# A deep trunk in exact fp32 halves: one block's turn shared by two engines, high parts first, and two steps of the last head in another order

## The chip, the cores and the metric

One core of one Trainium2 chip. The metric is the device time of one execution in microseconds, lower is better. TensorE (PE) multiplies, ScalarE (ACT), VectorE (DVE) and GpSimd (POOL) do the elementwise work, SyncE (SP) and the other engines' queues start DMA transfers. The kernel before ran in 942.38 us, median of three runs.

## The reference

Two layers of a decoder trunk over `S` = 512 tokens of width `D` = 1024, in fp32. Layer 0 mixes tokens by causal pooling, layer 1 by causal differential attention; a SwiGLU feed-forward network (inner width 2816) follows each; every residual is normalized afterwards.

```python
for i in range(2):
    if i % 2 == 0:
        h = multiscale_pool(x, pool_w, pool_scale)      # means over 2, 4, 8, 16 tokens minus x, times 4 matrices
    else:
        h = diff_attention(x, w_qkv, w_o, lam_p, subln_g, rel_table, lambda_init)   # 8 heads, 2 maps each
    x = layernorm(ALPHA * x + h, ln_mix_g[i], ln_mix_b[i])
    x = layernorm(ALPHA * x + (silu(x @ w_gate[i]) * (x @ w_up[i])) @ w_down[i], ln_ffn_g[i], ln_ffn_b[i])
```

## The kernel before

**Products.** Each fp32 operand is divided into a high part (a cast to the fast matmul format, `fp32r`, on ScalarE) and a low part (operand minus high part, on VectorE): `split` (L116, its two instructions L123 and L124). `mm3` (L147) makes a product of three matmuls: high by high (L149), high by low (L150), low by high (L151). In the profile a matmul's row names its line and its two inputs; `w3h` and `w3l` are the high and low parts of weight row 3.

**Weights.** All weights lie in one array of rows of 128x1024. `fetch` (L107) loads rows on SP's queue into five buffers (`raw`), `ready(n)` (L126) divides all rows up to n: for each it fetches five rows ahead, casts and subtracts. Rows 0 and 1 are the pooling matrices; rows 2 to 5 (`w2` to `w5`) are the gate and up matrices of the first two pairs of the feed-forward network, rows 6 and 7 (`g_4`, `g_5`) those of the third. The rows of the output matrix `w_o` of attention are `w92` to `w99`.

**Order.** The whole kernel is written in program order: the schedule is manual, so each engine runs its own instructions in the order in which the lines below issue them, and waits by semaphores for the others. Eight PSUM banks (`bank`, L62) are handed out by the framework as they come free.

**Start and pooling layer (L281 to L490).** Seven warm matmuls of the identity (`warm`, L324; an fp32 matmul is two records in the profile) fill TensorE until data are there. Tokens lie in four blocks of 128. `low` (L368) multiplies block 0 and 1 by the pooling bands, for each of eight column blocks k in turn: high by high, high by low, low by high; `d` (L285) is the correction for the first 16 tokens. `mixed(s, d)` (L401) multiplies pooled block s by the pooling matrices, `summed(s, d)` (L419) adds the result to the residual (`residual`, L181) and takes the statistics of the half row (`stat`, L187), `spread_of` (L194) gets mean and factor (the power is GpSimd's, L199), and `norm` (L202) normalizes.

**The turn.** The feed-forward products need the tokens along the free axis: `transposed(n, s)` (L232) turns block s by eight transposes into two PSUM banks (`pt`), and `turned` (L241) takes each bank in turn: four activations with the norm's scale and bias per partition write `y` (L249), then `split` writes the high and low parts into `xt`. Column blocks 0 to 3 come from the first bank, 4 to 7 from the second.

**Hand-over to the feed-forward network.** After the turns of block 0 and 1, `ffn(0, ...)` (L502) starts products for three gate/up pairs on the first half of the tokens (blocks 0 and 1; `lo` = 0), each product 24 matmuls of 256 columns, and goes on with the second half (`lo` = 256). The turns of blocks 2 and 3 are put between the products of the first half by `late`: after product (0, 1) and after product (1, 0), where (f, i) is pair f, i = 0 for gate (`g`), 1 for up (`u`). `product` (L623) calls `mm3` for k = 0 to 7.

**The last head (L1339 to L1417).** Attention runs head by head: `scores`, `softmax` (L1154), `combine` (L1170, the difference of the two maps), then one head later `transposed`, `mix` (values, with a square on ScalarE for the head norm), `root` (L1218: Ln and Exp on ScalarE) and `scaled` (L1228: the head's output times its factor on VectorE, then its division into parts). After head 7, `gather` (L1235) multiplies the first four heads by the first four rows of `w_o` for the four blocks s, and between these run `root(6)`, the transposes and `mix` of head 7, and `root(7)`. At block 0 `ready` divides row `w96` and then `scaled(6)` runs; at block 3 `ready` divides `w98` and `w99` and then `scaled(7)` runs.

Of the kernel before, what the change touches and what calls it, by code (L numbers as in the profile page):

```python
# [54 lines left out]
def trunk(ctx, tc, x, wall, pscale, lam_p, subln, table, lng, lnb, band, first, onehot, out):  # L55
# [60 lines left out]
    def split(dst_h, dst_l, src, scale=1.0, low=None):  # L116
        if scale != 1.0:
            nc.scalar.mul(dst_h, src, scale)
            nc.vector.scalar_tensor_tensor(
                dst_l, src, scale, dst_h.bitcast(F32), op0=ALU.mult, op1=ALU.subtract  # L120
            )
        else:
            nc.scalar.copy(dst_h, src)  # L123
            (low or nc.vector).tensor_tensor(dst_l, src, dst_h.bitcast(F32), op=ALU.subtract)  # L124
# [116 lines left out]
    def turned(n, s, kept=None):  # L241
        for i, pt in enumerate(turns.pop((n, s))):
            if kept:
                y = kept[i][:, :, s % 2 * P : (s % 2 + 1) * P]
            else:
                y = keep.tile([P, 4, P], F32, tag="y", name=f"y{n}_{s}_{i}", bufs=2)
            for k in range(4):
                kk = 4 * i + k
                nc.scalar.activation(  # L249
                    y[:, k, :],  # L250
                    pt[:, k * P : (k + 1) * P],
                    AF.Identity,
                    bias=bT[:, n, kk : kk + 1],
                    scale=gT[:, n, kk : kk + 1],
                )
            o = (s % 2) * P
            split(*(xt[:, s // 2, j, 4 * i : 4 * i + 4, o : o + P] for j in range(2)), y)

    def turn(n, s):
        transposed(n, s)  # L260
        turned(n, s)
# [19 lines left out]
    with tc.tile_pool(name="pool", bufs=1) as pp:  # L281
# [39 lines left out]
        sch = pp.tile([1, D], F32R, name="sch")  # L321
        scl = pp.tile([1, D], F32R, name="scl")
        warm = bank("warm")
        for i in range(7):  # L324
            nc.tensor.matmul(warm[:, 0:P], ident, ident, start=True, stop=True)
        scb = []
        nc.vector.tensor_copy(fh[:, :, :BAND], bnd)
# [28 lines left out]
        def xk(t, s, k):  # L356
            return t[:, s, k * P : (k + 1) * P]
# [8 lines left out]
                mm(scb[c], one, scl[:, cc], start=False, stop=True)  # L366

        def low(t, ks):  # L368
            for k in ks:
                g = k // 2  # L370
                o = made[0, g][:, (k % 2) * 256 : (k % 2 + 1) * 256]
                if t == 0:
                    mm(o, xk(xnh, 0, k), fh[:, g, :], start=k % 2 == 0, stop=False)
                    mm(o, xk(xnh, 0, k), fl[:, g, :], start=False, stop=False)
                    mm(o, xk(xnl, 0, k), fh[:, g, :], start=False, stop=False)
                else:
                    mm(o, xk(xnh, 1, k), bh[:, g, 0:256], start=False, stop=False)
                    mm(o, xk(xnl, 1, k), bh[:, g, 0:256], start=False, stop=k % 2 == 1)

        def high(blocks, ks):  # L380
            for s in blocks:
# [71 lines left out]
        tbh = pp.tile([33, HEADS], F32R, name="tbh")  # L453
        tbl = pp.tile([33, HEADS], F32R, name="tbl")
        ohr = pp.tile([33, NEAR], F32R, name="ohr")
        split(tbh, tbl, tb)
        nc.scalar.copy(ohr, oh_)
        transposed(0, 0)
# [4 lines left out]
        mm(lines_bank[:HEADS], tbl, ohr, start=False, stop=True)  # L463
        summed(1, 0, 1)
        spread_of(0, 1)
        summed(2, 0)
        norm(0, 1)
        transposed(0, 1)
        mixed(3, 1)
        turned(0, 0)  # L470
        summed(2, 1)
        spread_of(0, 2)
        turned(0, 1)
        ready(4)
        summed(3, 0, 1)
        norm(0, 2)
        spread_of(0, 3)
        ready(5)
        norm(0, 3)
        ready(6)  # L480

        line = pp.tile([HEADS, LINE], F32, name="line")
        far = pp.tile([HEADS, 1], F32, name="far")
        nc.gpsimd.memset(line[:, NEAR:], 0.0)
# [17 lines left out]
    def ffn(layer, late):  # L502
# [5 lines left out]
        with tc.tile_pool(name=f"ffn{layer}", bufs=1) as fp:  # L508
# [111 lines left out]
                if upto > len(chunks):  # L620
                    prepare(upto - len(chunks), upto - len(chunks))

            def product(acc, j, lo, hi):  # L623
                h, l = halves[j]
                for k in range(KB):
# [163 lines left out]
            load_terms(0)  # L789
            load_terms(1)  # L790
            sums = sums_of_x()
            for lo in (0, 256):
                for f in range(early):
                    for i in range(2):
                        product(accs[f][i], 2 * f + i, lo, lo + 256)
                        if not lo and (f, i) in late:
                            late[f, i]()
                        if not lo:
                            advance(2 * early, True)
                    if lo:  # L800
# [199 lines left out]
    def attention():  # L1000
        n = 2
        with tc.tile_pool(name="attn", bufs=1) as ap:
# [337 lines left out]
            for h in range(HEADS):  # L1340
                if h > 0:
                    combine(h - 1, 3)
                if h > 0:
                    split_values(h - 1)
                if h == 0:
                    scalars()
                if 1 < h <= SB + 1:
                    affine(n - 1, h - 2)
                if h == SB + 2:
                    load_gb(n)  # L1350
                if h + 1 < HEADS:
                    load_bias(h + 1)
                if h > 0:
                    accs = [bank(f"{nm}{h}") for nm in "qk"]
                    w = take(2)
                    ready(where[0] + {1: 3, last: 3}.get(h, 1))
                    query(accs[0], w[0])
                    split_query(h, "q", accs[0])
                    if h > 1:
                        root(h - 2)  # L1360
                    query(accs[1], w[1])
                    ready(where[0] + {1: 4, last: 3}.get(h, 2))
                    if h > 1:
                        scaled(h - 2)
                    split_query(h, "k", accs[1])
                    if h == 1:
                        w = take(2)
                        for r in range(2):
                            values("Q3", r, vc, w[r])
                        for s in range(2):  # L1370
                            combined(part(0, 1, s), vc[s], part(0, 1, s), ALU.subtract)
                    transposed(h - 1)
                start_scores(h)
                scores(h, 0, 1)
                for q in range(2):
                    softmax(h, q)
                if h == 0:
                    for s in range(2):
                        combined(part(1, 1, s), vc[s], part(1, 1, s), ALU.subtract)
                for q in (2, 3):  # L1380
                    scores(h, q)
                if h > 0:
                    mix(h - 1)
                if h == last:
                    ready(where[0] + 4)
                for q in (2, 3):
                    combine(h, q - 2)
                    softmax(h, q)
                combine(h, 2)
            cw = where[0]  # L1390
            combine(HEADS - 1, 3)
# [142 lines left out]
```

## Time and profile before

| | |
|---|---|
| Runs | 942.38, 941.96, 943.63 us; median 942.38 |
| Profiled execution | 942.9 us, span from first to last instruction 941.1 us |
| TensorE busy | 926.7 us, 98% of the span, 5712 matmuls |
| VectorE busy | 786.9 us, 84% |
| ScalarE busy | 514.2 us, 55% |
| GpSimd busy | 126.7 us, 13% |
| Mean granted TensorE clock | 0.997 |
| DMA | 211.11 MB, mean 224 GB/s |

How to read it: the busy times are sums over the whole execution, so they say which engine has least room, not what it waits for at one place; that is read from rows in order of time. Start times in rows are microseconds from the first instruction. Matmuls overlap in the record (a row lasts until its results are written), so the distance of their starts is what one costs. `L235` is a transpose, `L373` to `L378` are `low`'s matmuls, `L1160` the softmax's first pass on VectorE, `L1175` a step of `combine`.

### The profile page before, as it was taken

Reading aid. Unit: us, or ns where it says so; the run is one execution under the profiler, and the core shown is the slowest. Engines: PE = TensorE matmul, PEld = TensorE weight load, DVE = VectorE, ACT = ScalarE, POOL = GpSimd, SP = SyncE. Lnnn points to the kernel's source line nnn. Section 1 sums busy time; section 2 is a strip of 40 time slices with the busy share of each in tenths; the row PEclk is TensorE's granted clock in tenths of the full one; section 3 lists DMA queues with packets and bytes.
Section 4 is the critical chain, followed back from the end, with each engine's and each line's share of the span. In section 5 each row is a group of like instructions: output and inputs, shape, how many; then the busy total and the mean of one; then the engine's idle time right before and its main releaser. Section 6 shows DMA issues by size and latency. Waiting matters only on the chain.

```text
span 941.1 us, 14941 instructions
## 1 busy us (share of the span) xinstructions
PE 926.7 (98%) x5712; PEld 828.5 (88%) x5712; DVE 786.9 (84%) x1158; ACT 514.2 (55%) x819; POOL 126.7 (13%) x152
## 2 busy tenths in 40 slices
PE   9999999999999999999999999999999999999996
PEld 8898899999988888888888878988899999988884
DVE  7859979999988687868988876788789999987678
ACT  6652345555554457676878854743345554654450
POOL 4120120110101201201111100211111110001101
PEclk9999999999999999999999999999999999999998
DMA  9387998986868988976666612497888895878942
GB/s 236 124 254 249 341 284 245 249 255 211 266 203 266 367 264 238 221 196 159 157 145 168 159 57 88 138 321 225 262 246 261 250 278 197 258 247 282 350 163 91
DMA packets 86038, 211.11 MB, mean 224 GB/s; under 512 B 15140, under 2 KB 26660, under 8 KB 85966
## 3 DMA queue, kind: packets, MB, share of 16 engines
q1 hardware_dynamic: 43420, 117.16, 38.0%
q0 software_dynamic: 18768, 58.20, 25.1%
q10 hardware_dynamic: 23778, 34.78, 10.2%
q8 instruction: 45, 0.74, 0.3%
q14 instruction: 27, 0.22, 0.1%
HBM read 173.40 MB, written 36.72 MB: 223 GB/s over the span
## 4 chain that ended last, share of the span: by engine, by line
PE 89%; DVE 6%; ACT 3%; issue 1%; POOL 0%; DVEq 0%; ACTq 0%; POOLq 0%
PE A L859 17%; PE P L926 14%; PE C L859 9%; PE Q L926 6%; PE B L859 4%; PE g L151 3%; PE u L151 3%; PE u L149 3%; PE u L150 3%; PE g L149 3%; PE g L150 3%; PE s L1145 2%; PE va L1076 2%; PE q L149 1%; PE q L151 1%; PE k L149 1%
## 5 line engine op out<-in xcount | busy, mean ns | idle before, releaser
L605 DVE TENSOR_TENSOR raw<-raw,raw 128x1024 f32<-128x1024 f32 x56 | 68.2, 1219 | 0.5
L123 ACT CAST xs<-hid 128x512 fp32r<-128x512 f32 (+1 forms) x60 | 34.7, 581 | 24.3 <-DVE hid L773 24.3
L124 DVE TENSOR_TENSOR xs<-hid,xs 128x512 fp32r<-128x512 f32 (+1 forms) x60 | 38.3, 640 | 7.8 <-ACT xs L123 7.8
L1165 ACT ACTIVATE p<-p,mn 128x128 f32<-128x128 f32 (+3 forms) x64 | 35.2, 552 | 16.3 <-DVE mn L1160 16.3
L249 ACT ACTIVATE y<-pt,bT,gT 128x128 f32<-128x128 f32 x80 | 30.0, 455 | 19.4 <-PE pt L235 19.4
L704 POOL DMA_DIRECT2D b<-in_wall x20 | 14.0, 706 | 173.6 <-DMA tsum<-b 49.6
L765 POOL DMA_DIRECT2D xs<-ssum x24 | 17.4, 725 | 141.5 <-PE Q L926 68.2
L637 DVE TENSOR_TENSOR hid<-sg,u 128x512 f32<-128x512 f32 x16 | 10.9, 684 | 27.0 <-PE u L151 16.3
L199 POOL TENSOR_TENSOR rs<-rs,mhalf 128x1 f32<-128x1 f32 x16 | 12.9, 806 | 140.1 <-DVE rs L198 100.7
L704 POOL DMA_DIRECT2D hid<-in_wall x24 | 18.8, 824 | 78.9 <-DMA tsum<-hid 42.5
L1160 DVE CUSTOM_DVE_ANT_0 p<-s,bias 128x128 f32<-128x128 f32 (+3 forms) x64 | 28.0, 484 | 1.1 <-PE s L1145 1.1
L741 ACT CAST v<-u 128x512 fp32r<-128x512 f32 x22 | 13.7, 621 | 27.1 <-DVE u L739 27.0
L124 DVE TENSOR_TENSOR xt<-y,xt 128x512 fp32r<-128x512 f32 x20 | 13.6, 690 | 13.5 <-ACT xt L123 13.4
L190 DVE BATCH_NORM_STATS2 st<-res 128x6 f32<-128x512 f32 x32 | 22.2, 694 | 1.1
L885 ACT ACTIVATE sg<-sg 128x512 f32<-128x512 f32 x14 | 8.9, 633 | 25.7 <-DVE sg L878 25.7
L705 POOL DMA_DIRECT2D hid<-in_wall x12 | 14.8, 1233 | 56.0 <-DMA hid<-in_wall 56.0
L653 ACT CAST xs<-hid 128x1024 fp32r<-128x1024 f32 x8 | 8.4, 1050 | 24.0 <-DVE hid L670 11.6
L874 DVE TENSOR_TENSOR hid<-C,hid 128x512 f32<-128x512 f32 x14 | 9.7, 690 | 10.9 <-PE C L859 9.3
L1179 DVE SCALAR_TENSOR_TENSOR p<-p,sm,p 128x128 f32<-128x128 f32 (+3 forms) x32 | 17.6, 551 | 1.1
L870 ACT COPY hid<-C 128x512 f32<-128x512 f32 x14 | 8.2, 588 | 18.7 <-PE C L859 18.7
L705 POOL DMA_DIRECT2D b<-in_wall x10 | 12.3, 1230 | 38.1 <-DMA b<-in_wall 38.1
L124 POOL TENSOR_TENSOR sql<-sq,sqh 128x512 fp32r<-128x512 f32 x7 | 9.3, 1323 | 60.2 <-ACT sqh L123 60.2
(1187 smaller groups left out, 3673.2 us busy)
## 6 DMA issues: line engine op xcount, KB each, us to landing
raw<-in_wall SPq DMA_DIRECT2D x122, 512.0 KB, 5.2
r<-tsum SPq DMA_DIRECT2D x40, 512.0 KB, 4.4
hid<-in_wall POOLq DMA_DIRECT2D x36, 512.0 KB, 7.2
b<-in_wall POOLq DMA_DIRECT2D x30, 512.0 KB, 5.6
r<-in_wall SPq DMA_DIRECT2D x30, 512.0 KB, 4.7
tsum<-hid ACTq DMA_DIRECT2D x24, 512.0 KB, 5.7
ssum<-v ACTq DMA_DIRECT2D x22, 512.0 KB, 4.8
tsum<-b ACTq DMA_DIRECT2D x20, 512.0 KB, 5.1
```

The source lines that it names most:

```text
L123: nc.scalar.copy(dst_h, src)
L124: (low or nc.vector).tensor_tensor(dst_l, src, dst_h.bitcast(F32), op=ALU.subtract)
L149: nc.tensor.matmul(acc, ah, bh, start=start, stop=False)
L150: nc.tensor.matmul(acc, ah, bl, start=False, stop=False)
L151: nc.tensor.matmul(acc, al, bh, start=False, stop=stop)
L249: nc.scalar.activation(y[:, k, :], pt[:, k * P : (k + 1) * P], AF.Identity, bias=bT[:, n, kk : kk + 1], scale=gT[:, n, kk : kk + 1],)
L605: tt(t, raws[pair[0]], raws[pair[1]], op=ALU.add)
L704: nc.gpsimd.dma_start(out=t[:, j], in_=src[:, j])
L859: nc.tensor.matmul(o, w[:, c], x[:, kk, :], start=p in ("P1", "Q5", "P2") and f + kk + e == 0, stop=p in ("Q4", "Q3", "P2") and (f, kk, e) ...
L926: nc.tensor.matmul(accs[s], x[:, k, r], y[:, c], start=first and k == 0 and e == 0, stop=last and k == m - 1 and e == 2, skip_group_check= ...
L1160: nc.vector.tensor_tensor_reduce(out=p, in0=accs[c], in1=biases[h][:, w - 1 :: -1] if w < S else biases[h][:, ::-1], op0=ALU.add, op1=ALU. ...
L1165: nc.scalar.activation(p, p, AF.Exp, bias=mn[:, q, c : c + 1], scale=-1.0, accum_out=sm[:, q, c : c + 1],)
```

## The change

Six edits.

1. `turned_apart`, a new function, replaces `turned` for block 1. ScalarE takes the first bank: four activations write the high parts straight into `xt`. VectorE takes the second bank: four `tensor_scalar` write `y`, which ScalarE casts; then VectorE writes `y` of the first bank too, and then the two low parts, the second bank's first.
2. The order around it: the statistic of block 2's first half, the rest of its sum and its spread go behind block 1's turn and row 3 (`ready(4)`); rows 4 and 5 are divided one normalization earlier; the memset of `line` goes to the front of GpSimd's work.
3. The six products of the first half of the tokens in layer 0 are ordered by parts: all high by high, then high weights by low tokens, then low weights; the very first one by halves of k so that the low parts of the tokens come last. Blocks 2 and 3 are turned one product later.
4. `low` goes by parts as well, for four column blocks at a time, and there are six warm matmuls instead of seven (12 records).
5. In attention, `combine(h, 0)` and, for the last head, the row `w95` (`ready(where[0] + 4)`) come ahead of `mix(h - 1)`.
6. At blocks 0 and 3 of the first `gather`, `scaled` comes ahead of `ready`.

```diff
+    def turned_apart(n, s):
+        o = (s % 2) * P
+        pts = turns.pop((n, s))
+        ys = [
+            keep.tile([P, 4, P], F32, tag="y", name=f"y{n}_{s}_{i}", bufs=2) for i in range(2)
+        ]
+        hs, ls = (
+            [xt[:, s // 2, j, 4 * i : 4 * i + 4, o : o + P] for i in range(2)] for j in range(2)
+        )
+
+        def affine_of(i, k):
+            kk = 4 * i + k
+            return pts[i][:, k * P : (k + 1) * P], bT[:, n, kk : kk + 1], gT[:, n, kk : kk + 1]
+
+        def in_full(i):
+            for k in range(4):
+                a, bias, scale = affine_of(i, k)
+                nc.vector.tensor_scalar(
+                    ys[i][:, k, :], a, scalar1=scale, scalar2=bias, op0=ALU.mult, op1=ALU.add
+                )
+
+        for k in range(4):
+            a, bias, scale = affine_of(0, k)
+            nc.scalar.activation(hs[0][:, k, :], a, AF.Identity, bias=bias, scale=scale)
+        in_full(1)
+        nc.scalar.copy(hs[1], ys[1])
+        in_full(0)
+        for i in (1, 0):
+            nc.vector.tensor_tensor(ls[i], ys[i], hs[i].bitcast(F32), op=ALU.subtract)
...
-        for i in range(7):
+        for i in range(6):
             nc.tensor.matmul(warm[:, 0:P], ident, ident, start=True, stop=True)
...
         def low(t, ks):
-            for k in ks:
...
+            parts = ((xnh, fh), (xnh, fl), (xnl, fh)) if t == 0 else ((xnh, bh), (xnl, bh))
+            for d in range(2):
+                for e, (a, b) in enumerate(parts):
+                    for k in ks[4 * d : 4 * d + 4]:
...
+        nc.gpsimd.memset(line[:, NEAR:], 0.0)
...
-        summed(2, 0)
+        residual(2, 0, mixes[2][0])
         norm(0, 1)
         transposed(0, 1)
         mixed(3, 1)
         turned(0, 0)
+        turned_apart(0, 1)
+        ready(4)
+        stat(0, 2, 0)
         summed(2, 1)
         spread_of(0, 2)
-        turned(0, 1)
-        ready(4)
+        ready(5)
+        norm(0, 2)
         summed(3, 0, 1)
-        norm(0, 2)
         spread_of(0, 3)
-        ready(5)
+        ready(6)
         norm(0, 3)
-        ready(6)
...
+            ks = [range(4 * b, 4 * b + 4) for b in range(2)]
+            by_part = [(0, 0, range(KB)), (0, 1, range(KB)), (1, 0, range(KB))]
+            by_half = [(0, 0, ks[0]), (1, 0, ks[0]), (0, 0, ks[1]), (1, 0, ks[1])]
+            by_half += [(0, 1, ks[1]), (0, 1, ks[0])]
...
-                        product(accs[f][i], 2 * f + i, lo, lo + 256)
+                        product(
+                            accs[f][i], 2 * f + i, lo, lo + 256,
+                            None if layer or lo else by_part if f or i else by_half,
+                        )
...
+                combine(h, 0)
+                if h == last:
+                    ready(where[0] + 4)
                 if h > 0:
                     mix(h - 1)
-                if h == last:
-                    ready(where[0] + 4)
-                for q in (2, 3):
-                    combine(h, q - 2)
-                    softmax(h, q)
+                softmax(h, 2)
+                combine(h, 1)
+                softmax(h, 3)
                 combine(h, 2)
...
-                ready(cw + min(5 + s, WBUFS) if s < 3 else cw + 8)
                 if s in (0, 3):
                     scaled(last - 1 if s == 0 else last)
+                ready(cw + min(5 + s, WBUFS) if s < 3 else cw + 8)
...
-    ffn(0, {(0, 1): later(0, 2), (1, 0): later(0, 3)})
+    ffn(0, {(1, 0): later(0, 2), (1, 1): later(0, 3)})
```

In `by_part` and `by_half` an entry is (part of the weight, part of the tokens, column blocks), 0 for high and 1 for low.

More of the change, by code (lines that the diff above doesn't have):

```diff
@@ L368, in low @@
         def low(t, ks):
-            for k in ks:
[L370 to L378, printed above, removed]
+            parts = ((xnh, fh), (xnh, fl), (xnl, fh)) if t == 0 else ((xnh, bh), (xnl, bh))
+            for d in range(2):
+                for e, (a, b) in enumerate(parts):
+                    for k in ks[4 * d : 4 * d + 4]:
+                        g = k // 2
+                        mm(
+                            made[0, g][:, (k % 2) * 256 : (k % 2 + 1) * 256],
+                            xk(a, t, k), b[:, g, 0:256], start=t == e == k % 2 == 0,
+                            stop=t == 1 and e == 1 and k % 2 == 1, skip_group_check=True,
+                        )
         def high(blocks, ks):
@@ L455, in trunk @@
         ohr = pp.tile([33, NEAR], F32R, name="ohr")
+        line = pp.tile([HEADS, LINE], F32, name="line")
+        far = pp.tile([HEADS, 1], F32, name="far")
+        nc.gpsimd.memset(line[:, NEAR:], 0.0)
         split(tbh, tbl, tb)
@@ L470, in trunk @@
         turned(0, 0)
+        turned_apart(0, 1)
+        ready(4)
+        stat(0, 2, 0)
         summed(2, 1)
         spread_of(0, 2)
-        turned(0, 1)
-        ready(4)
+        ready(5)
+        norm(0, 2)
         summed(3, 0, 1)
-        norm(0, 2)
         spread_of(0, 3)
-        ready(5)
+        ready(6)
         norm(0, 3)
-        ready(6)
-        line = pp.tile([HEADS, LINE], F32, name="line")
-        far = pp.tile([HEADS, 1], F32, name="far")
-        nc.gpsimd.memset(line[:, NEAR:], 0.0)
         nc.scalar.copy(far, lines_bank[:HEADS, NEAR - 1 :])
@@ L621, in ahead, with product @@
                     prepare(upto - len(chunks), upto - len(chunks))
-            def product(acc, j, lo, hi):
+            def product(acc, j, lo, hi, apart=None):
                 h, l = halves[j]
+                if apart:
+                    for i, (w, e, ks) in enumerate(apart):
+                        for k in ks:
+                            nc.tensor.matmul(
+                                wide(acc, lo, hi), (h, l)[w][:, k * P : (k + 1) * P],
+                                x_at(k, lo, hi)[e], start=i == 0 and k == ks[0],
+                                stop=i == len(apart) - 1 and k == ks[-1],
+                            )
+                    return
                 for k in range(KB):
@@ L794, in ffn @@
                     for i in range(2):
-                        product(accs[f][i], 2 * f + i, lo, lo + 256)
+                        product(
+                            accs[f][i], 2 * f + i, lo, lo + 256,
+                            None if layer or lo else by_part if f or i else by_half,
+                        )
                         if not lo and (f, i) in late:
```

## The prediction

> **What bounds the kernel now.** I read the page's sums first, then the busy time by stretches, then the waits of TensorE in order of time.
>
> ```profile
> span 941.1 us, 14941 instructions
> PE 926.7 (98%) x5712; PEld 828.5 (88%) x5712; DVE 786.9 (84%) x1158; ACT 514.2 (55%) x819; POOL 126.7 (13%) x152
> 54.30:538.00 483.70, 483.31 (x2914) 427.38 (x2913) 410.09 (x643) 285.13 (x471) 65.65 (x75) 1.00 0.79 231
> ```
>
> TensorE is the bound: 926.7 of 941.1 us. Between 54.3 and 538 us it is idle for 0.4 us in 484. So a microsecond won ahead of 54.3 should reach the end, unless a later wait eats it, and no matmul, weight load or transpose is removed but two warm steps. The change can only take idle time of TensorE away or add some. What there is of it sits at three places: the first matmuls, the hand-over from the pooling layer to the first gate and up products, and the last head.
>
> (The third row is a stretch: its length, then busy time and instructions of PE, PEld, DVE, ACT, POOL, and the clock, DMA share and GB/s.) The hand-over, on TensorE (columns: start, duration, engine, line, operation, output and inputs, idle before and what ended it):
>
> ```profile
> 30.03 1.06 PE L235 MATMUL pt<-ident,res 128*128 128x128 f32 x8 [0.54 <-DVE res L208]
> ...
> 32.24 0.28 PE L151 MATMUL mix<-pw1h,pooled 128*128 128x256 f32 x1
> 32.90 0.39 PE L149 MATMUL g<-xt,w2h 128*128 128x256 f32 x1 [0.38 <-ACT xt L123]
> 37.10 0.28 PE L149 MATMUL u<-xt,w3h 128*128 128x256 f32 x1
> 44.72 1.03 PE L235 MATMUL pt<-ident,res 128*128 128x128 f32 x8
> 54.23 0.28 PE L149 MATMUL g<-xt,w2h 128*128 128x256 f32 x1
> ```
>
> From the turn of block 3 (44.72) to the second half of the tokens (54.23) TensorE has one turn of eight transposes and 72 matmuls, 9.51 us; from the turn of block 1 (30.03) to the end of the twelve mixing matmuls (32.24 and one step) one turn and 12, 2.33 us. The difference is 60 matmuls in 7.18: **0.12 each, and 0.89 a turn**. From 30.03 to 54.23 lie 3 turns and 156 matmuls, 21.4 us of work in 24.2 us. So 2.8 us are waits, and 0.5 more lie ahead of 30.03. More than 3.3 us can't be won here.
>
> VectorE and ScalarE in the same stretch (the first row is a stretch again):
>
> ```profile
> 29.08:43.18 14.10, 11.96 (x90) 10.61 (x89) 11.80 (x21) 8.84 (x18) 2.56 (x3) 1.00 0.17 42
> 27.90 0.55 POOL L199 TENSOR_TENSOR rs<-rs,mhalf 128x1 f32<-128x1 f32 x1 [4.44 <-DVE rs L198]
> 28.47 0.69 DVE L190 BATCH_NORM_STATS2 st<-res 128x6 f32<-128x512 f32 x1
> 29.08 0.80 DVE L208 TENSOR_SCALAR res<-res,mv,rs 128x1024 f32<-128x1024 f32 x1
> ...
> 35.88 1.23 DVE L124 TENSOR_TENSOR w3l<-raw,w3h 128x1024 fp32r<-128x1024 f32 x1 [0.25 <-ACT w3h L123]
> 37.03 0.68 DVE L183 SCALAR_TENSOR_TENSOR res<-res,mix 128x512 f32<-128x512 f32 x1
> ...
> 42.37 0.81 DVE L208 TENSOR_SCALAR res<-res,mv,rs 128x1024 f32<-128x1024 f32 x1 [0.44 <-POOL rs L199]
> 30.69 1.51 ACT L249 ACTIVATE y<-pt,bT,gT 128x128 f32<-128x128 f32 x4 [0.81 <-PE pt L235]
> ```
>
> Before, ScalarE does the affine and the cast of both banks of block 1's turn, and VectorE, waiting for it, is busy for 11.80 of 14.10 us.
>
> **The hand-over after the change.** *Statistic of block 2 moved.* The normalization of block 1 stands at 29.08 behind the statistic of 28.47; its factor is there at 27.90 + 0.55 = 28.45. Without the statistic it starts at 28.5, and with the 0.2 us of the start (below) at 28.3. TensorE's turn followed it by 0.95 (29.08 to 30.03), so it starts at 29.25, and twelve mixing matmuls end at 31.6.
>
> *Turn of block 1.* ScalarE began 0.66 after the turn did (30.69 against 30.03): now 29.9 to 31.4, four activations that write the high parts of the first bank directly. The first product goes by halves, high parts first, so it needs no more than that: it starts at 31.6, without the wait of 32.90. VectorE has the second bank: four TENSOR_SCALAR from PSUM, then four more of the first bank for the low parts. The trace has no such row from PSUM; the nearest:
>
> ```profile
> L1175 DVE TENSOR_SCALAR p<-p,sm,nlam 128x128 f32<-128x128 f32 x8 | 2.8, 347 | 0.3
> L1175 DVE TENSOR_SCALAR p<-p,sm,nlam 128x512 f32<-128x512 f32 x8 | 4.4, 547 | 0.3
> L1160 DVE CUSTOM_DVE_ANT_0 p<-s,bias 128x128 f32<-128x128 f32 x16 | 3.9, 283 | 1.1 <-PE s L1145 1.1
> L1160 DVE CUSTOM_DVE_ANT_0 p<-s,bias 128x512 f32<-128x512 f32 x16 | 10.4, 684 | 0.0
> ```
>
> The first form has the same two scalars per partition but reads SBUF, at (547 - 347) / 3 = 67 ns for 128 columns; the second reads PSUM, at (684 - 283) / 3 = 134. So the new one is about 347 + 67 = 414 ns, of which some 70 overlap the next (the normalization of 0.80 at 29.08 gave way to the next group after 0.72; by the rows above 35.88 + 1.23 gave way at 37.03, 0.08 early): **0.34 a piece, 2.75 for eight**. From below 0.21 (283 less the same overlap), from above 0.41: 1.7 to 3.3 for eight. I take the middle one, since the new form carries the two scalars of the dearer row. [...]
>
> *VectorE's chain is then the bound.* From block 1's to block 3's normalization it has the 11.80 us of before and the wait of 0.44 for GpSimd's factor, which keeps its place; new in the stretch are the moved statistic (0.62 in a chain), the low part of w5, now ahead of the last normalization (1.15, as 35.88 to 37.03), and 2.75: 16.8. From 28.3 this ends at 45.1; ScalarE's cast of block 0 adds about 0.1: 45.2. (Before: 43.18, at which TensorE was still 1.5 us from needing it.) Block 3's turn follows 0.15 later, at 45.35, then 0.89 for it and 48 matmuls at 0.12, 5.76: the second half starts at **52.0 instead of 54.23, 2.2 us sooner**. TensorE alone would be there at 29.25 + 21.4 = 50.65. On the way it waits a few tenths for the low parts of block 1 (the pieces of VectorE end around 33.1, the low parts at 33.8 and 34.4, wanted at 33.5 and 34.0) and for w5's (ready at 44.0, wanted at 43.4). With 0.21 a piece the gain is 3.3, with 0.41 it is 1.6.
>
> *What else moves.* Rows w3, w4, w5 keep their order; their loads are queued on SP behind the low parts that free a buffer, and these come at nearly the old times. Blocks 2 and 3 are turned one product later, since their normalizations come later; their high and low parts are wanted at 52.0 and end about 5.5 after block 3's turn starts (four activations and a cast twice, one low part), at 50.8. Cover 1.2 us. The memset of `line` moves ahead of GpSimd's powers, so ScalarE's DMA of `lines` no longer waits behind the last of them: off the path.
>
> **The start.**
>
> ```profile
> 1.91 3.36 PE L325 MATMUL warm<-ident 128*128 128x128 f32 x14 [1.91 <-POOL ident masks.py:199]
> 4.72 0.24 ACT L123 CAST fh<-d 16x64 fp32r<-16x64 f32 x1 [0.20 <-DMA d<-in_first]
> 5.01 0.58 PE L373 MATMUL pool<-fh,xt 128*128 128x256 f32 x1
> 5.42 0.58 PE L374 MATMUL pool<-fl,xt 128*128 128x256 f32 x1
> ...
> 6.83 0.28 PE L374 MATMUL pool<-fl,xt 128*128 128x256 f32 x1
> 6.94 0.28 PE L375 MATMUL pool<-fh,xt 128*128 128x256 f32 x1
> ```
>
> A step costs 0.24 in the warm run and 0.11 from 6.83. The first pooling matmul waits for the cast of `d`, over at 4.96, so two warm steps less (0.5) leave it at 5.01. The second came 0.41 later, waiting for a low part; by high parts first it has other work: 0.2 us won, at most 0.3, at least 0.
>
> **The last head.**
>
> ```profile
> 547.20 1.47 DVE L124 TENSOR_TENSOR w95l<-raw,w95h 128x1024 fp32r<-128x1024 f32 x1 [3.70 <-ACT w95h L123]
> 555.49 0.98 PE L1190 MATMUL at<-ident,p 128*128 128x128 f32 x7 [0.19 <-DVE p L1179]
> ...
> 557.47 0.40 PE L151 MATMUL wo<-w95h,heads 128*128 128x512 f32 x1
> 558.45 0.47 PE L149 MATMUL wo<-w92h,heads 128*128 128x512 f32 x1 [0.58 <-DVE rso L1230]
> ...
> 570.04 0.63 ACT L1225 ACTIVATE rso<-rso 128x512 f32<-128x512 f32 x1
> 570.58 1.03 ACT L123 CAST w98h<-raw 128x1024 fp32r<-128x1024 f32 x1
> 571.64 1.23 DVE L124 TENSOR_TENSOR w98l<-raw,w98h 128x1024 fp32r<-128x1024 f32 x1 [3.61 <-ACT w98h L123]
> 573.23 0.39 PE L149 MATMUL wo<-w98h,xt 128*128 128x512 f32 x1
> 573.46 0.39 PE L150 MATMUL wo<-w98l,xt 128*128 128x512 f32 x1
> 582.52 0.39 PE L151 MATMUL wo<-w99h,xt 128*128 128x512 f32 x1
> 583.00 0.44 PE L235 MATMUL pt<-ident,res 128*128 128x128 f32 x2
> ```
>
> VectorE stood 3.70 us for w95's cast, which ScalarE had put behind head 6's square. With the cast ahead of it the softmax of head 7 moves up by over 2 us, and the 0.19 ahead of its transposes goes. Head 6's scaling, now ahead of w96's row, no longer holds TensorE at 558.45: that step took 0.98 where a step is 0.23 (573.23 to 573.46): 0.75. The same edit also puts head 7's scaling ahead of rows w98 and w99, and that one costs: the exponential ends at 570.67, then VectorE's scaling (0.75, by the 0.68 of the form at 37.03 and a little), ScalarE's cast of its result (0.6, by the activation of this size at 570.04), w98's cast (1.03) and its low part (1.23), to 574.3. TensorE wants it at 573.46: **0.9 lost**. Of that 0.25 comes back at 583.00, where TensorE stood 0.48 - 0.23 for a normalization that then is early. Net: 0.19 + 0.75 - 0.9 + 0.25 = 0.3 won, between -0.5 (the gain at 558.45 is another buffer's) and 1.2 (the loss is covered). In the other heads the order on VectorE stays.
>
> **Sum.** 2.2 + 0.3 = 2.5 us (the start is within the 2.2). The profiled execution took 942.9, its span and 1.8 around it, 0.5 above the median of the three runs, 942.38; the runs spread from 941.96 to 943.63. The same difference off the median gives 939.9. What a measurement can tell from no change is 0.2%, 1.9 us: faster means below 940.5.
>
> **Rivals.** *The clock comes late.* TensorE's full rate began about 4.8 us after its first warm step (1.91 to 6.7). If the new pause ahead of 5.01 started that run anew, full rate would come at 9.8, 3.1 us more at half rate: 1.5 lost, 941.4, the same within the bound. Against: the pause is 0.2 to 0.4 us, and the old start had pauses as well. [...] 0.08.
>
> *VectorE eats it.* At 0.45 a piece or more beside ScalarE's reads, or with a second wait in its chain, the hand-over gives 1.3 or less: 941.2, the same. For it: the chain has no slack left at all. 0.16.
>
> *A bank is held.* Eight PSUM banks are shared, and the residuals of blocks 2 and 3 that free the mixing banks come later now. If the first `u` product (now at 34.9) were given the bank of block 3's first half, it would wait for that residual: 37.71 to 43.18 was 5.47, less block 2's normalization of 0.72, which no longer lies between, so 4.75 ahead of 45.2, at 40.4. From there TensorE has 120 matmuls and two turns: 40.4 + 14.4 + 1.8 = 56.6, 2.4 later than before, 944.5 with the last head: slower. It decides from a bank free after 38.0. Against: the old `u` product ran at 37.10, while that residual ended at 37.71 (37.03 + 0.68), so it had another bank, and those of block 0's turn and of block 2's first half are free by then. 0.06.
>
> **The numbers.** Forecast 0.66 (its own range 938.8 to 940.5), the others as given, 0.04 for a loss in what follows 54.3, where VectorE is busy 85% of the time. Faster 0.66; same 0.24; slower 0.10. With 0.21 a piece and the loss at 573.46 covered 938.1, which I take as unlikely; the low end is 938.5. Upward the range takes in both cases of no change: 942.3.
>
> **What would show it.** Right: TensorE's first `g` matmul near 31.6 without a wait, eight TENSOR_SCALAR from PSUM at about 0.41, the second half of the tokens at 52, the last turn waiting for block 3's normalization, no wait at the step of 558.45, a new one of about 0.9 at w98l. Wrong: the second half after 53, the full rate after 7.5, or new waits between 54 and 538.

## Result, and the profile after

| | before | after |
|---|---|---|
| Median of 13 runs each | 942.83 us (941.84 to 943.63) | 940.17 us (939.60 to 941.55) |
| Profiled execution | 942.9, span 941.1 | 940.0, span 938.2 |

The ratio is 0.9977, 95% interval 0.9968 to 0.9985: 2.7 us faster by the medians, 2.9 by the two profiled executions. Forecast were 939.9 and a gain of 2.5.

The page of the kernel after, and the long stretch (columns as before):

```profile
span 938.2 us, 14939 instructions
PE 925.0 (99%) x5710; PEld 827.2 (88%) x5710; DVE 789.8 (84%) x1166; ACT 512.9 (55%) x814; POOL 126.7 (14%) x152
51.90:538.00 486.10, 485.72 (x2929) 429.39 (x2928) 412.61 (x647) 288.54 (x475) 65.50 (x75) 1.00 0.79 231
```

TensorE is idle for 0.38 us in the 486 after the hand-over, against 0.39 in 484 before: nothing of what was won is given back there. TensorE through the hand-over, after the change:

```profile
31.08 0.64 PE L659 MATMUL g<-xt,w2h 128*128 128x256 f32 x4
...
32.52 0.64 PE L659 MATMUL g<-xt,w2l 128*128 128x256 f32 x4
33.14 1.34 PE L659 MATMUL g<-xt,w2h 128*128 128x256 f32 x8
...
40.87 2.15 PE L659 MATMUL u<-xt,w5h 128*128 128x256 f32 x16
43.86 1.21 PE L659 MATMUL u<-xt,w5l 128*128 128x256 f32 x8 [0.83 <-DVE w5l L124]
45.20 1.06 PE L235 MATMUL pt<-ident,res 128*128 128x128 f32 x8
...
51.85 0.28 PE L149 MATMUL g<-xt,w2h 128*128 128x256 f32 x1
```

The first product starts at 31.08 with no wait in its row, where 32.90 had one. The matmuls with the low tokens (33.14) come 0.14 later than four steps of 0.12 (the distance of two starts, as 32.04 and 32.52 for four) behind 32.52 would end. What is left are two places where TensorE stands behind VectorE: the wait for `w5l`, and the turn of block 3 at 45.20. The second half starts at 51.85 instead of 54.23, 2.38 sooner; not all of that is won in the hand-over (markers below). VectorE and GpSimd in the same stretch, and the group of the new instruction (count, then busy and mean ns):

```profile
27.79 0.81 DVE L208 TENSOR_SCALAR res<-res,mv,rs 128x1024 f32<-128x1024 f32 x1
28.52 1.40 DVE L124 TENSOR_TENSOR xt<-y,xt 128x512 fp32r<-128x512 f32 x2
29.85 2.64 DVE L276 TENSOR_SCALAR y<-pt,gT,bT 128x128 f32<-128x128 f32 x8
32.41 1.28 DVE L287 TENSOR_TENSOR xt<-y,xt 128x512 fp32r<-128x512 f32 x2
...
38.77 0.81 DVE L208 TENSOR_SCALAR res<-res,mv,rs 128x1024 f32<-128x1024 f32 x1 [0.44 <-POOL rs L199]
42.58 1.23 DVE L124 TENSOR_TENSOR w5l<-raw,w5h 128x1024 fp32r<-128x1024 f32 x1
44.24 0.81 DVE L208 TENSOR_SCALAR res<-res,mv,rs 128x1024 f32<-128x1024 f32 x1 [0.44 <-POOL rs L199]
37.32 1.41 POOL L199 TENSOR_TENSOR rs<-rs,mhalf 128x1 f32<-128x1 f32 x1 [9.57 <-DVE rs L198]
L276 DVE TENSOR_SCALAR y<-pt,gT,bT 128x128 f32<-128x128 f32 x8 | 2.6, 403 | 0.0
```

Eight `TENSOR_SCALAR` from PSUM take 29.85 to 32.41, 2.56, or 0.32 each. From block 1's normalization to block 3's VectorE's rows have no wait but two of 0.44 for GpSimd's factor.

The last head, after:

```profile
552.42 1.25 PE L1237 MATMUL at<-ident,p 128*128 128x128 f32 x10
...
554.67 0.39 PE L151 MATMUL wo<-w95h,heads 128*128 128x512 f32 x1
554.90 0.39 PE L149 MATMUL wo<-w92h,heads 128*128 128x512 f32 x1
...
567.08 0.75 DVE L1277 SCALAR_TENSOR_TENSOR rso<-o,gcol,rso 128x512 f32<-128x512 f32 x1 [2.67 <-ACT rso L1272]
568.39 1.04 ACT L123 CAST w98h<-raw 128x1024 fp32r<-128x1024 f32 x1
569.47 1.23 DVE L124 TENSOR_TENSOR w98l<-raw,w98h 128x1024 fp32r<-128x1024 f32 x1 [0.26 <-ACT w98h L123]
569.60 0.40 PE L149 MATMUL wo<-w98h,xt 128*128 128x512 f32 x1
570.75 0.50 PE L150 MATMUL wo<-w98l,xt 128*128 128x512 f32 x1 [0.75 <-DVE w98l L124]
```

The forecast wait at `w98l` is there: a step of 1.15 where one without a wait takes 0.23 (554.67 to 554.90). Two long steps of before are gone. One is the 0.98 at head 6's scaling (now 554.67 to 554.90, 0.23); the other is one of 0.47 within head 7's transposes, which now run ten in a row. From the first `wo` product to `w100` the part takes 51.55, against 52.02 before.

### The profile page after: what moved, and what is told of

It is laid out like the page before. It is cut to its first block, busy times and chain, and to the rows that moved or that the text cites. A ratio compares the mean times of both kernels' runs of the same rounds, so it can differ in the third digit from the quotient of the medians.

```text
span 938.2 us, 14939 instructions
## 1 busy us (share of the span) xinstructions
PE 925.0 (99%) x5710; PEld 827.2 (88%) x5710; DVE 789.8 (84%) x1166; ACT 512.9 (55%) x814; POOL 126.7 (14%) x152
## 4 chain that ended last, share of the span: by engine, by line
PE 92%; DVE 5%; ACT 1%; issue 1%; DMA 0%; POOL 0%; DVEq 0%; ACTq 0%; POOLq 0%
PE A L906 17%; PE P L973 14%; PE C L906 9%; PE Q L973 6%; PE B L906 4%; PE g L150 3%; PE u L150 3%; PE g L149 3%; PE u L151 3%; PE u L149 3%; PE g L151 3%; PE s L1192 2%; PE va L1123 2%; PE wo L150 1%; PE wo L151 1%; PE q L149 1%
## 5 line engine op out<-in xcount | busy, mean ns | idle before, releaser
L249 ACT ACTIVATE y<-pt,bT,gT 128x128 f32<-128x128 f32 x72 | 27.1, 456 | 26.6 <-PE pt L235 23.5
```

Source lines behind the costliest of these rows:

```text
L249: nc.scalar.activation(y[:, k, :], pt[:, k * P : (k + 1) * P], AF.Identity, bias=bT[:, n, kk : kk + 1], scale=gT[:, n, kk : kk + 1],)
```

## Experiments

Three markers of the profiled executions are used below. `lines` is TensorE's only product of that name, ahead of the hand-over (28.86 before, 28.17 after); H is the time from it to the second half of the tokens (25.37 before, 23.68 after); W is the time from the first `wo` product to `w100`'s. "Onset" is where the distance of matmul starts in the first pooling products halves (6.76 before, 5.33 after): before, it is 0.22 at 6.01 and 0.12 at 6.94. "Half rate" at the start means these longer steps; the granted clock in the record reads 1.00 there as well (0 to 12 us, before and after). H and W hold nothing of the start. The kernel before was run again beside the experiments: its median was 942.68 beside the three parts and the run with head 7's scaling put back, 942.70 beside the doubled scalars, the old order of parts and the two kernels with a bank for each engine, and 942.38 beside the last three. One kernel's median thus differs by some tenths from group to group, so finer comparisons go by H and W.

### The parts alone

The kernel before with edits 1 to 3 (the turn, the order, the products by parts), with edit 4 alone (the start), and with edits 5 and 6 alone (the last head).

> The kernel before with the hand-over's edits alone (block 1's turn by two engines, the new order around it, products by parts, blocks 2 and 3 turned one product later); 14 warm records, the old order of the first pooling matmuls and the old last head. Theory: the change won 2.4 us up to the second half of the tokens, and at most 0.1 of it is the start's, so this one wins 1.9 to 2.4 against the kernel before (0.9975 to 0.998) and its second half starts 1.9 to 2.4 us ahead of the 54.23 of before, less or more by the time at which the clock came up. Rival (the start counts, with its 0.7 us at the pooled lines): 1.2 to 1.7 won.

> The kernel before with 12 warm records and the first pooling matmuls by high parts, nothing else. Theory: what the profile of the change showed at the start (0.7 us) was the time at which the clock came up in that execution, 5.33 against 6.76 us, which is a matter of each execution; with the half rate before that time taken out, the start wins 0.1 us or less, and the time is the same, within 0.5 us. Rival: fewer warm records bring the clock up sooner or leave less to do at half rate, 0.5 to 0.7 won. Rival on the other side: the pause ahead of the first pooling matmul delays the clock, 1 to 1.5 lost in part of the executions.

> The kernel before with the last head's edits alone. Theory: 1.2 us won up to the row w96, 0.9 lost at w98's low part, 0.2 regained at the next turn: 0.4 to 0.6 won, a ratio of 0.9994 to 0.9996. Rival: the two gains at head 6 don't last, no difference or 0.4 lost.

| | median (runs) | ratio to before, 95% | H | W |
|---|---|---|---|---|
| before, same chip | 942.68 (27) | | 25.37 | 52.02 |
| edits 1 to 3 | 940.73 (11) | 0.998, 0.9971 to 0.9989 | 23.69 | 52.05 |
| edit 4 | 942.53 (11) | 0.9998, 0.9989 to 1.0006 | 25.36 | 52.04 |
| edits 5, 6 | 942.33 (11) | 0.9993, 0.9984 to 1.0002 | 25.34 | 51.55 |

The hand-over carries 1.95 of the gain; H is that of the whole change to 0.01. The start has no effect that the runs show. The last head's 0.47 shows in W alone; its interval of times takes in no change. By the medians the three add up to 2.45, by H and W to 2.2.

### Is VectorE the bound?

The eight `tensor_scalar` are each issued a second time, which repeats work and changes no value:

```diff
+        in_full(1)
         in_full(1)
         nc.scalar.copy(hs[1], ys[1])
+        in_full(0)
         in_full(0)
```

> The changed kernel with VectorE's eight TENSOR_SCALAR of block 1's turn run twice (the same values, written again). Theory: VectorE's chain up to block 3's normalization is what the second half of the tokens waits for, without slack, so eight more at 0.32 a piece put the turn of block 3 from 45.2 to 47.8 and the second half from 51.85 to 54.4: 2.6 us lost against the change, about 942.7, as long as the kernel before. Rival: the gain of the hand-over is the order of the products on TensorE, and VectorE has room in it: less than 0.7 lost.

VectorE and TensorE of this kernel:

```profile
29.95 5.20 DVE L276 TENSOR_SCALAR y<-pt,gT,bT 128x128 f32<-128x128 f32 x16
...
46.91 0.81 DVE L208 TENSOR_SCALAR res<-res,mv,rs 128x1024 f32<-128x1024 f32 x1 [0.44 <-POOL rs L199]
33.30 0.74 PE L661 MATMUL g<-xt,w2h 128*128 128x256 f32 x4 [1.01 <-ACT xt L285]
...
35.80 1.82 PE L661 MATMUL g<-xt,w2h 128*128 128x256 f32 x8 [1.28 <-DVE xt L289]
37.42 3.10 PE L661 MATMUL u<-xt,w3h 128*128 128x256 f32 x16
40.36 1.11 PE L661 MATMUL u<-xt,w3l 128*128 128x256 f32 x8
...
47.95 1.04 PE L235 MATMUL pt<-ident,res 128*128 128x128 f32 x8
...
54.57 0.28 PE L149 MATMUL g<-xt,w2h 128*128 128x256 f32 x1
```

943.0 us, ratio 1.0003 (0.9994 to 1.0012): 2.54 more VectorE work ahead of `w3l` put block 3's normalization 2.67 later and the second half 2.72 later, and the whole gain is gone. But TensorE was late by itself here too: its first product waited 1.01 + 1.28 = 2.3 us, and then 24 matmuls took from 35.80 to 40.36, 4.56 us where 24 steps of 0.12 are 2.88. Its products end just as VectorE lets block 3's turn go: there is no wait ahead of 47.95. So the run shows the price of dearer pieces, 1 us for each us, but not which of the two chains would have taken it alone. That VectorE bounds is shown the other way round, by the kernels further down in which it has less to do or wait for.

### Products in the old order of parts

```diff
-                            None if layer or lo else by_part if f or i else by_half,
+                            None,
```

> The changed kernel with the first half's products in the old order (for each k high by high, high by low, low by high), all else kept. Theory: the first product then waits for the first bank's low part, which VectorE ends around 33.7: its second matmul stands at 33.8 instead of 31.2, the products end 2.5 later, at about 46.6, and block 3's turn, which VectorE allowed at 45.2, starts 1.4 late: 1.4 us lost, about 941.6, more than half of the hand-over's gain. Rival (the order of the parts only fills time in which TensorE waits for VectorE anyway): less than 0.4 lost.

```profile
32.31 0.28 PE L149 MATMUL g<-xt,w2h 128*128 128x256 f32 x1
34.98 0.39 PE L150 MATMUL g<-xt,w2h 128*128 128x256 f32 x1 [2.39 <-DVE xt L287]
...
37.17 0.41 PE L149 MATMUL g<-xt,w2h 128*128 128x256 f32 x1
37.38 0.41 PE L150 MATMUL g<-xt,w2h 128*128 128x256 f32 x1
...
45.49 0.81 DVE L208 TENSOR_SCALAR res<-res,mv,rs 128x1024 f32<-128x1024 f32 x1 [0.44 <-POOL rs L199]
36.40:38.00 1.60, 1.60 (x9) 0.50 0.52 133
```

(The last row is a stretch with TensorE alone: length, busy, clock, DMA share, GB/s.) The second matmul waits 2.55 for the low tokens. H is 26.06, 2.38 more than after, where 1.4 was expected. VectorE's chain is where it was (45.49 is 16.09 behind `lines`; after, 16.07), so TensorE lost it by itself. From its first product to the second half it loses 4.1 us against 0.12 a step: 2.55 in the wait and 1.55 behind it, where a step takes 0.21 (37.17 to 37.38) for 3.4 us, 35.4 to 38.8, and the granted clock is 0.50 (the last row). The kernel after loses 1.7 in the same part, and the difference is the 2.4. The median is 941.65, 1.5 above after. Its ten runs lie in two groups, 940.82 to 941.28 and 942.03 to 944.44; the profiled one (943.23) is in the upper. The lower group is 0.8 above after, which is what would be left without the half clock (2.55 - 1.7). That the clock is what divides the groups is guessed from one profile, not shown.

### Block 1 turned by ScalarE alone, the rest kept

```diff
-        turned_apart(0, 1)
+        turned(0, 1)
```

> The changed kernel with block 1's turn by the old function (ScalarE does both banks, VectorE only the low parts); the products by parts, the moved statistic and everything else kept. Theory: VectorE loses eight TENSOR_SCALAR (2.6 us) but waits for ScalarE's second cast (about 33.6, in place of 31.9) and for w3's cast behind it, so w3's low part starts at 34.6 in place of 33.6 and the whole chain up to block 3's normalization is 1.0 late: 1.0 lost against the change, about 941.2. So sharing the turn is worth about 1 us of the hand-over's 2.3, and the order the rest. Rival: the sharing is the whole of it, 2 us or more lost. Rival: the eight instructions cost VectorE what they save, no difference.

```profile
32.51 0.75 PE L659 MATMUL g<-xt,w2h 128*128 128x256 f32 x4 [0.39 <-ACT xt L123]
...
34.56 0.74 PE L659 MATMUL g<-xt,w2h 128*128 128x256 f32 x4 [0.84 <-ACT xt L123]
```

H is 24.71: 1.03 of the 1.69 won is lost, as expected. Both halves of the first product wait for ScalarE's cast, and VectorE waits for ScalarE's casts as well (1.69 and 1.37 ahead of the two low parts, 0.26 ahead of `w3l`), so that `w3l` starts at 35.50. The time is 940.77, 0.6 above after (1.6 below the kernel before beside it, where the whole change won 2.7). With everything else in place, sharing the turn is thus worth 1.0 of the 1.7 in the trace. The other 0.7 is the order of the products and of VectorE's work together, which no run takes apart: without the order of the products alone, the profiled execution loses more than all of H's gain (26.06 above), half clock included.

### Head 7's scaling behind the rows again

```diff
-                if s in (0, 3):
-                    scaled(last - 1 if s == 0 else last)
+                if s == 0:
+                    scaled(last - 1)
                 ready(cw + min(5 + s, WBUFS) if s < 3 else cw + 8)
+                if s == 3:
+                    scaled(last)
```

> The changed kernel with head 7's scaling behind rows w98 and w99 again, head 6's still ahead of w96. Theory: the wait of 0.75 for w98's low part goes, and TensorE wins 0.9 there, of which the next turn's wait of about 0.2 comes back: 0.6 to 0.7 us less than the change, 0.9970 against the kernel before. Rival: head 7's scaling was late in the kernel before and its parts are now what TensorE waits for at w99, so the time is that of the change, 0.9977.

939.50 (5 runs, 0.9963, 0.9950 to 0.9975), 0.67 below after, with intervals that overlap. W decides: it is 50.80, since the wait for `w98l` goes, and the old step of 0.48 ahead of the next transposes (block 0's, 583.00 before) comes back. The half of edit 6 for head 7 is a loss of 0.75 in W. The other half, for head 6, and edit 5 win 1.22 together (52.02 to 50.80); they were not run apart.

### A bank for each engine in full, another order, other starts

If VectorE is the bound, ScalarE, with room (busy 55% of the span), should do the first bank's `y` too, so that VectorE has four pieces and not eight; the kernel also has the edit of the last section.

```diff
-            nc.scalar.activation(hs[0][:, k, :], a, AF.Identity, bias=bias, scale=scale)
+            nc.scalar.activation(ys[0][:, k, :], a, AF.Identity, bias=bias, scale=scale)
         in_full(1)
-        nc.scalar.copy(hs[1], ys[1])
-        in_full(0)
-        for i in (1, 0):
+        for i in range(2):
+            nc.scalar.copy(hs[i], ys[i])
+        for i in range(2):
...
-            by_half += [(0, 1, ks[1]), (0, 1, ks[0])]
+            by_half += [(0, 1, ks[0]), (0, 1, ks[1])]
```

> The changed kernel with head 7's scaling late and with the turn shared in another way: ScalarE writes the first bank in full and casts both, VectorE does only the second bank's four TENSOR_SCALAR and both low parts. Theory (VectorE's chain is the bound): four TENSOR_SCALAR less, 1.3 us, of which about 0.4 goes into a wait for the first high part; the first product starts 0.4 later, at 31.5, and still the second half starts 0.8 to 0.9 sooner: 0.8 less than with head 7 late alone, about 938.7. Rival (TensorE's start is the bound): 0.4 lost against it.

```profile
30.20 1.37 DVE L276 TENSOR_SCALAR y<-pt,gT,bT 128x128 f32<-128x128 f32 x4
31.80 1.29 DVE L287 TENSOR_TENSOR xt<-y,xt 128x512 fp32r<-128x512 f32 x2 [0.23 <-ACT xt L285]
33.27 1.23 DVE L124 TENSOR_TENSOR w3l<-raw,w3h 128x1024 fp32r<-128x1024 f32 x1 [0.18 <-ACT w3h L123]
PE g L659 <- ACT xt L285: 0.4, 1, 0.4
PE pt L235 <- DVE res L208: 0.2, 1, 0.2
```

938.79 (5 runs, 0.9955, 0.9942 to 0.9967): 1.4 below after, the best of all, as expected. H is 23.17, 0.53 better than with eight pieces (23.70 in the kernel of the last section), where 0.8 to 0.9 was expected. VectorE's chain from block 1's normalization to block 3's is 0.51 shorter, 16.75 against 17.26, and that is the gain; the rest of the 1.3 that four pieces take went into VectorE's own waits for ScalarE, two of which are in the rows. The first product waits 0.4 for ScalarE's cast (the last two rows are TensorE's waits: total, times, longest), but that costs nothing here: the wait for `w5l` is gone, and the turn of block 3 still waits 0.2 for VectorE.

The next kernel also takes away GpSimd's wait ahead of block 2's normalization, by dividing `w4`'s row ahead of that block's last sums and putting block 3's residual behind them:

```diff
-        ready(4)
+        ready(5)
         stat(0, 2, 0)
         summed(2, 1)
         spread_of(0, 2)
-        ready(5)
+        residual(3, 0, mixes[3][0])
         norm(0, 2)
-        summed(3, 0, 1)
+        stat(0, 3, 0)
+        summed(3, 1)
         spread_of(0, 3)
```

> The same as the run before it, with the order behind the turn changed as well: row 4 divided directly behind row 3, block 3's first residual between block 2's factor and its normalization, so that VectorE reads PSUM instead of two SBUF operands while GpSimd takes the power. Theory: GpSimd's power takes 0.55 instead of 1.41 there, since in the traces it ends only behind VectorE's subtraction of a weight row, and VectorE's wait of 0.44 ahead of block 2's normalization goes: 0.4 us more won on VectorE's chain, of which TensorE can use 0.2 to 0.4; about 938.4. Rival: the power's time is GpSimd's own and the wait stays, no difference.

```profile
40.11 0.55 POOL L199 TENSOR_TENSOR rs<-rs,mhalf 128x1 f32<-128x1 f32 x1 [10.18 <-DVE rs L198]
39.88 0.68 DVE L183 SCALAR_TENSOR_TENSOR res<-res,mix 128x512 f32<-128x512 f32 x1
40.70 0.81 DVE L208 TENSOR_SCALAR res<-res,mv,rs 128x1024 f32<-128x1024 f32 x1
43.78 1.23 DVE L124 TENSOR_TENSOR w5l<-raw,w5h 128x1024 fp32r<-128x1024 f32 x1
45.45 0.81 DVE L208 TENSOR_SCALAR res<-res,mv,rs 128x1024 f32<-128x1024 f32 x1 [0.44 <-POOL rs L199]
5.37 1.22 PE L404 MATMUL pool<-fh,xt 128*128 128x256 f32 x4 [0.52 <-ACT fh L123]
...
8.95 1.05 PE L404 MATMUL pool<-fl,xt 128*128 128x256 f32 x4
9.80 0.68 PE L404 MATMUL pool<-fh,xt 128*128 128x256 f32 x4
```

H falls by another 0.43 to 22.74, a little more than expected: the power takes 0.55 (40.11), not the 1.41 that it took beside a division of a row, and the wait ahead of 40.70 is gone. The time is 938.84 (5 runs, 0.9959, 0.9947 to 0.9972), no better than the kernel ahead of it, where 938.4 was expected. In the profiled execution, the slowest of the five (940.42), the first four steps over 0.85 (8.95 to 9.80) show the half rate up to an onset of 9.91. I took the pause of 0.52 ahead of the first pooling matmul, longer than the 0.19 in the kernel after, for the reason, and tried 14 and 8 warm records in place of 12 in the same kernel. My forecasts were an onset of 4.8 to 8.3 and a median of 938.3 to 938.8, with the slowest run below 939.8, for 14, and an onset of 8.2 to 11.8 and a median of 940.0 to 940.6 for 8. They were estimates that rest on a guess of how such a pause delays the full rate, which no run had shown:

> The kernel with the shared turn, the new order and head 7 late, with 14 warm records in place of 12. [...] Rival: the number of warm records does nothing to the clock, as before, 938.8 with a slowest of 940.4.

> The same kernel with 8 warm records. [...]

| warm records | onsets in all profiled executions | this kernel's median |
|---|---|---|
| 14 | 6.76, 6.93, 7.44, 7.39 | 939.52 (5 runs, 937.82 to 939.92) |
| 12 | 5.33, 6.25, 6.11, 5.63, 8.10, 5.75, 9.91, 7.34 | 938.84 (5 runs, 938.34 to 940.42) |
| 8 | 10.94 | 940.01 (11 runs, 939.51 to 941.39) |

With 8 the onset is late, as expected. The time lies where it was forecast (940.0 to 940.6), but it is only 0.5 above that with 14, where 1.3 to 1.9 was expected, and these intervals overlap. With 14 the onset lies where it was expected but the time doesn't: 938.3 to 938.8 was forecast, and its slowest run isn't below 939.8. The two latest onsets, 9.91 and 10.94, are those of two executions with pauses of 0.52 and 0.92 ahead of the first pooling matmul; it was 0.19 in the kernel after, 0.25 with the old order of parts (onset 8.10) and 0.2 with a bank for each engine in full. That fits a pause that delays the full rate, by one execution each. That 12 records lose to 14 is not shown, rather the other way, with intervals that overlap. Two more records are no remedy.

## Why the prediction came out

**Which engine bounds, and where.** Right. TensorE's idle time between 52 and 538 stayed as it was, and the edits' gain came from the two places named: H gives 1.69, W 0.47. The other 0.69 of the span's 2.9 lies ahead of `lines` and goes with the earlier onset in this execution (below), which is luck. By the traces the edits are worth 2.2, by the medians 2.5 (the parts) to 2.7 (the whole), and 2.5 was forecast; the intervals of the medians can't tell these apart.

**The turn of block 1.** Right: the first product came 3.29 after block 1's normalization, forecast 3.3, and without a wait; that it stands at 31.08 and not at 31.6 goes with the earlier onset (5.33). A piece took 403 ns and 0.32 in the chain, against 414 and 0.34; eight took 2.56 of the forecast 2.75. Taking the fixed part of the dearer row held.

**VectorE's chain.** Right in kind, with one term missed. It ran 27.79 to 45.05, 17.26, where 28.3 to 45.2, 16.9, was forecast. The step "the wait of 0.44 for GpSimd's factor, which keeps its place" failed: there are two. The rows `w4` and `w5` are each divided one normalization earlier, so that now the factors of block 2 and of block 3 are both computed beside such a division, with 1.41 for the power in place of 0.55. Taking one away was worth 0.43. Pieces 0.19 cheaper made up for part of it, and the rest was hidden by luck: the chain started 0.5 earlier, with the earlier onset of this execution. So the turn of block 3 (45.20 against 45.35), the second half (51.85 against 52.0) and `w5l` (ready at 43.81 against 44.0) agree with the forecast better than its working did. Counted from `lines`, the second half came 1.69 sooner, where 2.2 less the 0.2 of the start, 2.0, was worked out.

**The start.** Its 0.69 in this execution goes with the onset: that came 1.43 sooner, and with steps of 0.12 in place of 0.22 to 0.24 half of that, some 0.71, would be gained. With half of the time from the first warm record (1.91) to the onset taken off, `lines` averages 0.06 earlier over the eight executions with 12 records (26.36) than over the three with the old start (26.42). The eight spread over 0.17, so the edit itself is worth 0.1 or nothing, where 0.2 was taken (0 to 0.3).

**The last head.** Right in sign and place, 0.47 for 0.3. Up to `w96` 1.25 was won where 0.19 + 0.75 was counted: the transposes' 0.19 of idle time was a step of 0.47 in place of 0.11, so 0.36 and not 0.19, and the steps right behind the two old waits are 0.06 and 0.08 shorter. The loss at `w98l` was 0.92 (0.9), and the step behind it 0.11 more; the 0.25 came back.

**The rivals.** The bank was not held (no such wait). *VectorE eats it* came half true: the second wait in its chain, which this rival named, is there. Its price was too high, since H still won 1.69 where the rival left 1.3 or less for the hand-over. Dear pieces would have done it: with all eight run twice the gain was gone. The full rate did not come late in the profiled execution, but it does in others: onsets with 12 records lie from 5.33 to 9.91, and half of the difference, 2.3, is more than the hand-over wins.

## What to carry to other kernels

A product that waits for an operand in a high and a low part can begin with all the high parts; it hides the making of the low ones (H is 23.68 with that order, 26.06 with the old one). In the run with the old order of parts, a wait of 2.4 us for the low ones was followed by 3.4 us at a granted clock of 0.50. When two engines share a step, count the pieces on the one that is already the bound: four pieces there instead of eight won 0.5 us more, though the other engine then did more. A wait that is to be carried over from the old order is counted anew in the new one, once for each place where its cause (here a division of a weight row beside GpSimd's power, 1.41 in place of 0.55) now stands.

## What the runs showed of the hardware

**Behind two long waits of TensorE stood a stretch of slow steps.** With the products in the old order, a wait of 2.39 was followed by 3.4 us of steps of 0.21 in place of 0.12, at a granted clock of 0.50, a loss of some 1.6 on top of the wait. With the doubled scalars, two waits of 1.01 and 1.28 in one product were followed by 24 matmuls in 4.56 us in place of 2.88, a loss of some 1.7. Behind waits of 0.39 and 0.84 in one product (block 1 turned by ScalarE alone) the steps were 0.12 (35.62 to 36.58 for eight). From what wait on the steps get longer, these runs leave open.

**The time at half rate at the start (steps of 0.21 to 0.24 in place of 0.12) varies by several us.** Onsets with 12 records, one execution each of eight kernels, spread over 4.6 us, half of which is 2.3. The runs of the kernel after alone spread over 1.95; that the onset makes this spread is not shown.

**GpSimd's power of 128x1 takes 0.55 or 1.41 us by what VectorE does beside it.** At 40.11 above it ran beside the residual, whose second input is PSUM; at 37.32 in the kernel after beside a subtraction of two SBUF operands, and ended some 0.4 behind it (38.73 against 38.32). The difference is 0.86 us; what causes it, the runs do not show.
